# Row sums of 1024 floats on one core: two row blocks of 112 and 16 with a store each, and a last row added by two chained pair instructions on VectorE

## Chip, cores, metric

The kernel runs on one core of a Trainium2 chip. The metric is the time of one execution on the device in microseconds (us), lower is better. The profile shows a span that is about 1.8 us shorter than the time of the same execution, so differences of spans and of times can be compared.

## The reference

```python
def setup_inputs():
    batch, seq, dim = 32, 512, 1024
    return {"x": np.random.randn(batch, seq, dim).astype(np.float32)}

def reference(x):
    return np.sum(x, axis=-1).astype(np.float32)
```

That is 16,384 rows of 4 KB: 67.1 MB to read and 64 KB to write. Every element is added once, so the kernel is a test of how steadily one core can load.

## The kernel before

The rows are cut into four blocks. In a block each of the 128 partitions owns 32 consecutive rows, so the rows of neighbouring partitions lie 32 x 4 KB = 128 KB apart in memory. A load brings 16 rows a partition (64 KB in one piece from each partition's rows, 8 MB in all) into one of three buffers. VectorE sums 16 rows in one instruction. After each of the first three blocks, ScalarE's queue issues a store of 32 sums a partition (128 bytes).

```python
BLOCKS = (32, 32, 32, 32)
G = 16
ACT_ROWS = 6
CUT = 640
# ... pools: three buffers of 16 rows for x; one buffer for each result
    for b, n in enumerate(BLOCKS):
        x_b, out_b, res = block(done * P, n)
        final = b == len(BLOCKS) - 1
        whole = n - G if final else n
        c = 0
        while c < whole:
            m = min(G, whole - c)
            xt = xpool.tile([P, G * D], F32, tag="xt", name="xt")
            nc.sync.dma_start(out=xt[:, 0 : m * D], in_=x_b[:, c * D : (c + m) * D])
            a = ACT_ROWS if done + c + m == full else 0
            rows_dve(xt, res, 0, m - a, c)
            rows_act(xt, res, m - a, a, c + m - a)
            c += m
        if not final:
            nc.scalar.dma_start(out=out_b, in_=res)
        done += n
```

The last 16 rows come in pieces of 8, 4, 2 and 1 rows and the last row in pieces of 640 and 384 elements, so that little work is left when the last byte lands. VectorE and ScalarE share the rows of each piece. The end of the last row:

```python
    nc.vector.tensor_reduce(
        out=tail[:, D : D + 1], in_=tail[:, 0 : CUT // 2], axis=X, op=ADD
    )
    sum_act(tail[:, CUT // 2 : CUT], tail[:, D + 1 : D + 2])
    nc.vector.tensor_reduce(
        out=res[:, n - 1 : n], in_=tail[:, CUT : D + 2], axis=X, op=ADD
    )
    nc.sync.dma_start(out=out_b, in_=res)
```

`pairs_dve` (already used for the row before the last) is one VectorE instruction that adds the first half of a piece to the second half, sums the results and adds a start value: it covers n elements in n/2 steps (for the row of 1024 elements before the last the trace shows 692 ns).

Of the kernel before, what the change touches and what calls it, by code (L numbers as in the profile page):

```python
# [1 line left out]

# [4 lines left out]

F32 = mybir.dt.float32
ADD = mybir.AluOpType.add
COPY = mybir.ActivationFunctionType.Copy  # L10
X = mybir.AxisListType.X

BLOCKS = (32, 32, 32, 32)
G = 16
ACT_ROWS = 6
CUT = 640


@with_exitstack
def row_sums(  # L20
    ctx: ExitStack,
    tc: tile.TileContext,
    x: bass.AP,
    out: bass.AP,
):
    nc = tc.nc
    P = nc.NUM_PARTITIONS

    x_flat = x.flatten_outer_dims()
    R, D = x_flat.shape  # L30
    C = R // P
    assert R % P == 0 and sum(BLOCKS) == C
    out_flat = out.rearrange("a (b c) -> (a b c)", c=1)

    xpool = ctx.enter_context(tc.tile_pool(name="x", bufs=3))
    rpool = ctx.enter_context(tc.tile_pool(name="res", bufs=1))
    tail = rpool.tile([P, D + 2], F32, name="tail")

    def rows_dve(xt, res, j, n, c):
        nc.vector.tensor_reduce(  # L40
            out=res[:, c : c + n],
            in_=xt[:, j * D : (j + n) * D].rearrange("p (j d) -> p j d", d=D),
            axis=X,
            op=ADD,
        )

    def sum_act(v, acc):
        nc.scalar.activation(out=v, in_=v, func=COPY, accum_out=acc)  # L48

    def rows_act(xt, res, j, n, c):  # L50
        for i in range(n):
            sum_act(xt[:, (j + i) * D : (j + i + 1) * D], res[:, c + i : c + i + 1])

    def pairs_dve(xt, a, b, first, acc):
        h = (a + b) // 2
        nc.vector.tensor_tensor_reduce(  # L56
            out=xt[:, a:h], in0=xt[:, a:h], in1=xt[:, h:b], scale=1.0, scalar=first,
            op0=ADD, op1=ADD, accum_out=acc,
        )

    def block(r0, n):
        x_b = x_flat[r0 : r0 + P * n].rearrange("(p c) d -> p (c d)", p=P)
        out_b = out_flat[r0 : r0 + P * n].rearrange("(p c) -> p c", p=P)
        return x_b, out_b, rpool.tile([P, n], F32, name=f"res{r0}")

    full = C - G
    done = 0
# [18 lines that stand above are left out]
    cuts = [0, 8, 12, 14, 15]  # L86
    for i, k in zip(cuts, cuts[1:]):
        nc.sync.dma_start(out=xt[:, i * D : k * D], in_=x_b[:, (c + i) * D : (c + k) * D])
    last = (n - 1) * D
    nc.sync.dma_start(out=tail[:, 0:CUT], in_=x_b[:, last : last + CUT])  # L90
    nc.sync.dma_start(out=tail[:, CUT:D], in_=x_b[:, last + CUT : last + D])

    for i, k in zip(cuts[:2], cuts[1:3]):
        h = (k - i + 1) // 2
        rows_dve(xt, res, i, h, c + i)
        rows_act(xt, res, i + h, k - i - h, c + i + h)
    i = cuts[2]
    rows_dve(xt, res, i, 1, c + i)
    rows_act(xt, res, i + 1, 1, c + i + 1)
    i += 2  # L100
    pairs_dve(xt, i * D, (i + 1) * D, 0.0, res[:, c + i : c + i + 1])
    nc.vector.tensor_reduce(  # L102
        out=tail[:, D : D + 1], in_=tail[:, 0 : CUT // 2], axis=X, op=ADD
    )
    sum_act(tail[:, CUT // 2 : CUT], tail[:, D + 1 : D + 2])
    nc.vector.tensor_reduce(  # L106
        out=res[:, n - 1 : n], in_=tail[:, CUT : D + 2], axis=X, op=ADD
    )
    nc.sync.dma_start(out=out_b, in_=res)


def kernel(tc: tile.TileContext, x: bass.AP, out: bass.AP):
    row_sums(tc, x, out)
    tc.close()
    tc.compile()  # L115



    sp = mybir.EngineType.SP
    entry, body = None, None  # L120
    for blk in tc.nc.m.functions[0].blocks:
        ops = [i for i in blk.instructions if i.engine == sp]
        if entry is None:
            entry = blk
        elif any(i.opcode == "DMACopy" for i in ops):
            body = blk
            break
    code = list(body.instructions)
    load = next(i for i in code if i.engine == sp)
    assert load.opcode == "DMACopy" and not load.sync_info.on_wait  # L130
    code.remove(load)
    body.instructions = code
    code = list(entry.instructions)
    at = next(k for k, i in enumerate(code) if i.engine == sp and i.opcode == "Drain")
    code.insert(at, load)
    entry.instructions = code


# [1 line left out]
_INS = ['x']  # L140
_OUTS = [((32, 512), 'float32')]


# [23 lines left out]
```

## Time and profile before

| | before |
|---|---|
| time, median of 3 runs | 162.77 us (162.54 to 163.09) |
| span of the profiled execution | 161.35 us (its time: 163.13) |
| bytes loaded over the span | 416 GB/s |
| VectorE / ScalarE busy | 77% / 10% |
| load queue, share of the 16 DMA engines' span | 97.2% |

The page of the kernel before: its head, its busy engines and its DMA queues. q1 is the queue of the loads and the last store, q10 the queue on which ScalarE issues; the columns of a queue are packets, MB, and the time its packets took as a share of 16 engines' span.

```profile
span 161.3 us, 116 instructions
...
DVE 123.5 (77%) x14; ACT 15.8 (10%) x29; POOL 0.2 (0%) x4
...
q1 hardware_dynamic: 2016, 67.13, 97.2%
q10 hardware_dynamic: 432, 0.05, 0.2%
```

The loads leave the DMA engines idle for under 3% of the span, and VectorE is idle for a quarter of it. So the loads bound the kernel, and a change can only win what lies between the packets, before the first, or after the last.

VectorE's timeline of the kernel before, from the fourth load on (start, duration, engine, line, operation, tiles and shapes, and in brackets the idle time before it and what ended it):

```profile
80.01 17.22 DVE L40 TENSOR_REDUCE res<-xt 128x16 f32<-128x16384 f32 x1 [2.15 <-DMA xt<-in_x_dram]
99.57 17.22 DVE L40 TENSOR_REDUCE res<-xt 128x16 f32<-128x16384 f32 x1 [2.34 <-DMA xt<-in_x_dram]
119.30 17.22 DVE L40 TENSOR_REDUCE res<-xt 128x16 f32<-128x16384 f32 x1 [2.51 <-DMA xt<-in_x_dram]
138.73 18.46 DVE L40 TENSOR_REDUCE res<-xt 128x10 f32<-128x10240 f32 x4 [2.21 <-DMA xt<-in_x_dram]
```

Each of these starts when a load lands, so the differences of the starts are the times between landings: 19.56, 19.73 and 19.43 us here, and 19.34 to 19.37 for the loads before.

The end of the timeline of the kernel before:

```profile
157.95 0.47 ACT L48 ACTIVATE tail<-tail 128x320 f32<-128x320 f32 x1 [0.97 <-DMA tail<-in_x_dram]
157.95 0.49 DVE L102 TENSOR_REDUCE tail<-tail 128x1 f32<-128x320 f32 x1
158.33 0.19 ACT L48 ACTIVATION_READ_ACCUMULATOR tail<-tail 128x1 f32 x1
158.55 0.55 DVE L106 TENSOR_REDUCE res<-tail 128x1 f32<-128x386 f32 x1
159.13 0.35 SPq L109 DMA_DIRECT2D out_dram<-res  x1
```

and of its chain of waits, the work that ended last, in order of time (start, duration, what):

```profile
119.46 38.47 DMA tail<-in_x_dram
157.93 0.02 issue
157.95 0.47 ACT tail L48
158.42 0.10 ACTq L115
158.52 0.02 issue
158.55 0.55 DVE res L106
```

### The profile page before, as it was taken

The page shows a single profiled execution, that of the slowest core. Times are in us where ns is not written, and L with a number is a line of the kernel's source. Part 1 is how long each engine was busy: PE and PEld are TensorE (multiplying, and loading weights), DVE is VectorE, ACT ScalarE, POOL GpSimd, SP SyncE. Part 2 cuts the span into 40 slices and gives each one's busy share as a digit, 9 for nine tenths or more (in the row PEclk, how much of TensorE's full clock was granted, in tenths as well). Part 3 has the DMA queues.
Part 4 walks back from the last instruction along what each step waited for, and adds up shares of the span by engine and source line. Part 5 has one row for each costly group of instructions (what it writes and reads, how often), then busy time and mean ns, then how long its engine had stood idle before and what let it go on. Part 6 is the DMA issues. An engine that isn't in the chain of part 4 may idle for free.

```text
span 161.3 us, 116 instructions
## 1 busy us (share of the span) xinstructions
DVE 123.5 (77%) x14; ACT 15.8 (10%) x29; POOL 0.2 (0%) x4
## 2 busy tenths in 40 slices
DVE  0000059997799959999499994999949998699994
ACT  0000000000000000000000000000000000891881
POOL 0000000000000000000000000000000000000000
DMA  7995995996995995996996996997979969999991
GB/s 260 520 520 260 520 520 260 520 520 260 520 520 260 520 520 260 521 521 260 521 520 260 520 520 260 521 456 326 521 309 471 520 260 520 390 391 449 406 407 44
DMA packets 2448, 67.18 MB, mean 416 GB/s; under 512 B 784, under 2 KB 912, under 8 KB 1168
## 3 DMA queue, kind: packets, MB, share of 16 engines
q1 hardware_dynamic: 2016, 67.13, 97.2%
q10 hardware_dynamic: 432, 0.05, 0.2%
HBM read 67.11 MB, written 0.07 MB: 416 GB/s over the span
## 4 chain that ended last, share of the span: by engine, by line
DMA 76%; DVE 22%; ACT 0%; issue 0%; ACTq 0%
DMA xt<-in_x_dram 39%; DMA tail<-in_x_dram 24%; DVE res L40 21%; DMA out_dram<-res 14%; DVE res L106 0%; ACT tail L48 0%; ACTq L115 0%
## 5 line engine op out<-in xcount | busy, mean ns | idle before, releaser
L40 DVE TENSOR_REDUCE res<-xt 128x16 f32<-128x16384 f32 (+4 forms) x10 | 121.8, 12203 | 35.4 <-DMA xt<-in_x_dram 35.4
L48 ACT ACT_TABLE_LOAD x1 | 1.3, 1283 | 137.0 <-DVE res L40 137.0
L48 ACT ACTIVATE xt<-xt 128x1024 f32<-128x1024 f32 x13 | 13.6, 1045 | 4.8 <-DMA xt<-in_x_dram 4.8
L48 ACT ACTIVATION_READ_ACCUMULATOR xt<-xt 128x1 f32 x13 | 2.4, 186 | 0.0
L56 DVE CUSTOM_DVE_ANT_0 xt<-xt 128x512 f32<-128x512 f32 x1 | 0.7, 692 | 0.0
L106 DVE TENSOR_REDUCE res<-tail 128x1 f32<-128x386 f32 x1 | 0.6, 554 | 0.1
L48 ACT ACTIVATE tail<-tail 128x320 f32<-128x320 f32 x1 | 0.5, 470 | 1.0 <-DMA tail<-in_x_dram 1.0
L102 DVE TENSOR_REDUCE tail<-tail 128x1 f32<-128x320 f32 x1 | 0.5, 486 | 0.0
L48 ACT ACTIVATION_READ_ACCUMULATOR tail<-tail 128x1 f32 x1 | 0.2, 187 | 0.0
L151 POOL MEMSET const-uint8-127<- 128x1 uint8 x1 | 0.1, 103 | 0.0
L151 POOL MEMSET const-bfloat16-1.0<- 128x1 bf16 x1 | 0.1, 102 | 0.0
L151 POOL MEMSET const-float32-0.0<- 128x1 f32 x1 | 0.1, 99 | 0.2 <-issue 0.2
L151 POOL MEMSET const-float32-1.0<- 128x1 f32 x1 | 0.1, 99 | 0.0
L56 DVE DVE_READ_ACCUMULATOR2_ANT res<- 128x1 f32 x1 | 0.1, 84 | 0.0
## 6 DMA issues: line engine op xcount, KB each, us to landing
xt<-in_x_dram SPq DMA_DIRECT2D x1, 4096.0 KB, 31.6
xt<-in_x_dram SPq DMA_DIRECT2D x1, 2048.0 KB, 36.1
xt<-in_x_dram SPq DMA_DIRECT2D x1, 1024.0 KB, 38.1
xt<-in_x_dram SPq DMA_DIRECT2D x1, 512.0 KB, 38.9
tail<-in_x_dram SPq DMA_DIRECT2D x1, 320.0 KB, 38.5
tail<-in_x_dram SPq DMA_DIRECT2D x1, 192.0 KB, 38.6
xt<-in_x_dram SPq DMA_DIRECT2D x7, 41.0
out_dram<-res ACTq DMA_DIRECT2D x3, 16.0 KB, 22.2
```

The source lines that it names most:

```text
L40: nc.vector.tensor_reduce(out=res[:, c : c + n], in_=xt[:, j * D : (j + n) * D].rearrange("p (j d) -> p j d", d=D), axis=X, op=ADD,)
L48: nc.scalar.activation(out=v, in_=v, func=COPY, accum_out=acc)
L56: nc.vector.tensor_tensor_reduce(out=xt[:, a:h], in0=xt[:, a:h], in1=xt[:, h:b], scale=1.0, scalar=first, op0=ADD, op1=ADD, accum_out=acc,)
L102: nc.vector.tensor_reduce(out=tail[:, D : D + 1], in_=tail[:, 0 : CUT // 2], axis=X, op=ADD)
L106: nc.vector.tensor_reduce(out=res[:, n - 1 : n], in_=tail[:, CUT : D + 2], axis=X, op=ADD)
L151: nc = _bacc.Bacc("TRN2", target_bir_lowering=False, num_devices=1)
```

## The change

The intent: fewer and larger stores (112 sums a partition, 448 bytes, in place of three times 128 bytes), and a last row that only VectorE works on, with the first pair instruction between the two landings and the second after the last one. The row before the last goes to ScalarE.

```diff
-BLOCKS = (32, 32, 32, 32)
+BLOCKS = (112, 16)
 G = 16
 ACT_ROWS = 6
-CUT = 640
+CUT = 576
+EARLY = 1
...
-    tail = rpool.tile([P, D + 2], F32, name="tail")
+    part = rpool.tile([P, 1], F32, name="part")
...
-    last = (n - 1) * D
-    nc.sync.dma_start(out=tail[:, 0:CUT], in_=x_b[:, last : last + CUT])
-    nc.sync.dma_start(out=tail[:, CUT:D], in_=x_b[:, last + CUT : last + D])
+    last = 15 * D
+    for i, k in ((0, CUT), (CUT, D)):
+        nc.sync.dma_start(
+            out=xt[:, last + i : last + k],
+            in_=x_b[:, c * D + last + i : c * D + last + k],
+        )
 
-    for i, k in zip(cuts[:2], cuts[1:3]):
-        h = (k - i + 1) // 2
+    for i, k in zip(cuts[:3], cuts[1:4]):
+        h = (k - i) // 2
         rows_dve(xt, res, i, h, c + i)
-        rows_act(xt, res, i + h, k - i - h, c + i + h)
-    ...  (rows 12 to 15: ScalarE's and VectorE's halves, as shown above)
+        rows_act(xt, res, i + h, h, c + i + h)
+    rows_act(xt, res, 14, 1, c + 14)
+    pairs_dve(xt, last, last + CUT, 0.0, part)
+    pairs_dve(xt, last + CUT, last + D, part, res[:, c + 15 : c + 16])
     nc.sync.dma_start(out=out_b, in_=res)
```

The rest of the diff lets EARLY loads be issued ahead of the start barrier; with EARLY = 1 that is what the kernel did before. With 112 rows a partition, neighbouring partitions' rows now lie 448 KB apart instead of 128 KB. (The last 16 rows of a partition are a block of their own, so in the pieces at the end they lie 64 KB apart.)

More of the change, by code (lines that the diff above doesn't have):

```diff
@@ L88, in row_sums @@
         nc.sync.dma_start(out=xt[:, i * D : k * D], in_=x_b[:, (c + i) * D : (c + k) * D])
-    last = (n - 1) * D
-    nc.sync.dma_start(out=tail[:, 0:CUT], in_=x_b[:, last : last + CUT])
-    nc.sync.dma_start(out=tail[:, CUT:D], in_=x_b[:, last + CUT : last + D])
-    for i, k in zip(cuts[:2], cuts[1:3]):
-        h = (k - i + 1) // 2
-        rows_dve(xt, res, i, h, c + i)
-        rows_act(xt, res, i + h, k - i - h, c + i + h)
-    i = cuts[2]
-    rows_dve(xt, res, i, 1, c + i)
-    rows_act(xt, res, i + 1, 1, c + i + 1)
-    i += 2
-    pairs_dve(xt, i * D, (i + 1) * D, 0.0, res[:, c + i : c + i + 1])
-    nc.vector.tensor_reduce(
-        out=tail[:, D : D + 1], in_=tail[:, 0 : CUT // 2], axis=X, op=ADD
-    )
-    sum_act(tail[:, CUT // 2 : CUT], tail[:, D + 1 : D + 2])
-    nc.vector.tensor_reduce(
-        out=res[:, n - 1 : n], in_=tail[:, CUT : D + 2], axis=X, op=ADD
-    )
+    last = 15 * D
[6 more added lines that the diff above has]
+        h = (k - i) // 2
+        rows_dve(xt, res, i, h, c + i)
+        rows_act(xt, res, i + h, h, c + i + h)
+    rows_act(xt, res, 14, 1, c + 14)
+    pairs_dve(xt, last, last + CUT, 0.0, part)
+    pairs_dve(xt, last + CUT, last + D, part, res[:, c + 15 : c + 16])
     nc.sync.dma_start(out=out_b, in_=res)
@@ L128 @@
     code = list(body.instructions)
-    load = next(i for i in code if i.engine == sp)
-    assert load.opcode == "DMACopy" and not load.sync_info.on_wait
-    code.remove(load)
+    loads = [i for i in code if i.engine == sp][:EARLY]
+    for load in loads:
+        assert load.opcode == "DMACopy" and not load.sync_info.on_wait
+        code.remove(load)
     body.instructions = code
@@ L134 @@
     at = next(k for k, i in enumerate(code) if i.engine == sp and i.opcode == "Drain")
-    code.insert(at, load)
+    code[at:at] = loads
     entry.instructions = code
```

## The prediction

> **What bounds it now.** The 16 DMA engines. The page's queue part gives the load queue 97.2% of 16 engines' span; VectorE is busy 77%, ScalarE 10%. The packet records of the trace show 64 KB load packets of 2418 ns at the least, back to back: 4.19 MB an engine at that rate is 154.8 us of the 161.3 us span (estimate from those records). The rest: [...]0.8 us of longer first packets, 1.2 us of longer packets and gaps, and the end after the last landing (about 158.45): in the timeline the last reduce runs 158.55 to 159.10, its store is issued at 159.13, the span ends at 161.3. VectorE's 17.22 us for each 16-row load fits in the 19.4 us between landings. The bytes loaded don't change, so nothing large can be won.
>
> **What the change does.**
> 1. Three stores of 128-byte packets during the loads become one of 448-byte packets. The Trainium skill ("DMA: Bandwidth & Descriptors", Issuing engines are not separate DMA queues) says that DMAs issued from ScalarE interleave with others on the same 16 engines; the packet records agree: store packets of 13 ns between load packets, 8 an engine for each store[...]. That is 0.3 us an engine for three stores; one of larger packets should cost 0.1 to 0.15. Gain 0.15 to 0.2 us, on the critical path.
> 2. The end. Before, the last piece lands at about 158.45 and VectorE starts at 158.55, held by ScalarE's half of the 640 piece (157.95 to 158.52), and takes 0.55 us. After: the pairs on 288 elements, about 0.46 us (estimate: 692 ns for 512, so 1.04 ns an element and 160 fixed), fit between the two landings; the pairs on 224 need 0.40. The result is ready 0.15 to 0.2 us earlier.
> 3. The trap: the 112-row store stands in ScalarE's order behind its six rows and waits for VectorE's 10-row reduce (10.82 us, ends near 149.5). ScalarE's rows of the last 16, begun at 148.47 before, begin near 149.9. It has eight rows at 1.05 us, the last landing near 157.1, and ends near 158.4, half a microsecond before VectorE: off the critical path, with little slack.
> 4. Rows of neighbouring partitions lie 448 KB apart instead of 128 KB; the contiguous run stays 64 KB. The fifth and sixth loads now show packets of 2450 to 2456 ns against 2418 to 2426, which I can't explain; if it is the addresses, this may move half a microsecond either way.
> 5. ScalarE's table load leaves the end of the kernel: it was not on the chain.
>
> **Sum.** 162.77 - 0.17 - 0.18, about 162.4 us; range 161.7 to 163.0 (the three runs of before spread 162.54 to 163.09). Faster by over 2%: 0.01; within 2%: 0.98; slower: 0.01.
>
> **What would show it.** Load queue still about 97% busy; last landing 0.1 to 0.5 us earlier; landings 19.35 to 19.7 us apart; from the last landing to the last store's issue 0.45 us in place of 0.65; the big store landing within about 8 us of an issue near 149.9, before the last loads end; ScalarE's last read ending before VectorE's last pairs.
>
> **What would make it wrong.** The new row stride slows or speeds the packets of all loads (each 1% is 1.5 us); ScalarE, started late, ends last; the big store lands after the last loads and holds the end of the program; the second pairs wait for the first's sum longer than the two landings are apart.

The first packets start 0.99 to 1.51 us after the start of the span, and the three stores landed 23.9, 22.2 and 12.5 us after their issue.

## More of the kernel before

The chain does not run through the last piece of 384 elements (landed at 158.40) but through the piece before it, of 640: landed at 157.93, ScalarE's half of it, then the last reduce. From that landing to the issue of the last store are 1.20 us; from the landing of the last piece they are 0.73.

## The result

| | before | after |
|---|---|---|
| time, median of 4 runs | 162.66 us (162.46 to 163.09) | 162.46 us (162.34 to 162.61) |
| span of the profiled execution | 161.35 us | 160.83 us |
| load queue's share | 97.2% | 97.2% |
| rate over the span | 416 GB/s | 418 GB/s |

The ratio is 0.9985 with a 95% interval of 0.9962 to 1.0008. A ratio is the mean time of one kernel's fast runs over the mean of the other's fast runs of the same rounds, so it is not quite the ratio of the medians. The changed kernel run once more later, over five rounds on another chip, gave 0.9979 (0.9964 to 0.9994), so the gain is real: 0.2 to 0.35 us of 162.7.

The page after, the same parts:

```profile
span 160.8 us, 116 instructions
...
DVE 122.7 (76%) x14; ACT 16.1 (10%) x29; POOL 0.2 (0%) x4
...
q1 hardware_dynamic: 2016, 67.12, 97.2%
q10 hardware_dynamic: 144, 0.06, 0.1%
```

VectorE's timeline after, from the fourth load on:

```profile
80.06 17.22 DVE L41 TENSOR_REDUCE res<-xt 128x16 f32<-128x16384 f32 x1 [2.14 <-DMA xt<-in_x_dram]
99.42 17.22 DVE L41 TENSOR_REDUCE res<-xt 128x16 f32<-128x16384 f32 x1 [2.14 <-DMA xt<-in_x_dram]
118.76 17.22 DVE L41 TENSOR_REDUCE res<-xt 128x16 f32<-128x16384 f32 x1 [2.12 <-DMA xt<-in_x_dram]
138.11 18.46 DVE L41 TENSOR_REDUCE res<-xt 128x10 f32<-128x10240 f32 x4 [2.13 <-DMA xt<-in_x_dram]
```

The landings are now 19.36, 19.34 and 19.35 us apart. At 138.11 the changed kernel is 0.62 us ahead of the kernel before (138.73), and at the end of the span it is 0.52 us ahead. So in this pair of profiles the whole gain was made in the loads five to seven, before the new end began.

The timeline after: the big store on ScalarE's queue and what follows it, and the end.

```profile
149.02 0.37 ACTq L83 DMA_DIRECT2D out_dram<-res  x1
149.51 1.06 ACT L49 ACTIVATE xt<-xt 128x1024 f32<-128x1024 f32 x1 [3.69 <-DVE res L41]
...
157.50 0.46 DVE L57 CUSTOM_DVE_ANT_0 xt<-xt 128x288 f32<-128x288 f32 x1 [0.92 <-DMA xt<-in_x_dram]
157.75 0.19 ACT L49 ACTIVATION_READ_ACCUMULATOR xt<-xt 128x1 f32 x1
157.88 0.08 DVE L57 DVE_READ_ACCUMULATOR2_ANT part<- 128x1 f32 x1
158.01 0.45 DVE L57 CUSTOM_DVE_ANT_0 xt<-xt,part 128x224 f32<-128x224 f32 x1
158.39 0.08 DVE L57 DVE_READ_ACCUMULATOR2_ANT res<- 128x1 f32 x1
158.53 0.35 SPq L104 DMA_DIRECT2D out_dram<-res  x1
```

The chain of waits after, its end:

```profile
118.49 38.86 DMA xt<-in_x_dram
157.35 0.03 issue
157.38 0.02 DVEq L57
157.40 0.10 issue
157.50 0.46 DVE xt L57
157.95 0.02 DVE part L57
157.97 0.04 issue
158.01 0.45 DVE xt L57
```

Again the chain starts at the landing of the last row's first piece (157.35), and from there to the issue of the last store are 1.18 us. Before it was 1.20. The new end is not a shorter chain. It gains only because the first piece is smaller and so lands sooner: its packets took 93 to 94 ns against 102, eight of them on each engine, which is 0.07 us. Counted from the landing of the last piece, the store was issued after 0.66 us in place of 0.73. But even this was lost again after the last store: from the landing of the last piece to the end of the span both profiles have 2.95 us. Why is told under no_stores.

ScalarE did what was feared and no more: its store waited for VectorE until 149.02, its next row began at 149.51, and its last read ended at 157.94, half a microsecond before VectorE's last read. The big store landed 6.6 us after its issue.

### The profile page after: what moved, and what is told of

Same layout as the page of the kernel before. It is cut to its first block, busy times and chain, and to the rows that moved or that the text cites. A ratio compares the mean times of both kernels' runs of the same rounds, so it can differ in the third digit from the quotient of the medians.

```text
span 160.8 us, 116 instructions
## 1 busy us (share of the span) xinstructions
DVE 122.7 (76%) x14; ACT 16.1 (10%) x29; POOL 0.2 (0%) x4
## 3 DMA queue, kind: packets, MB, share of 16 engines
q1 hardware_dynamic: 2016, 67.12, 97.2%
## 4 chain that ended last, share of the span: by engine, by line
DMA 75%; DVE 22%; SPq 1%; issue 0%; DVEq 0%
DMA xt<-in_x_dram 75%; DVE res L41 21%; SPq L89 1%; DVE xt L57 1%; DVEq L57 0%; DVE part L57 0%; DVEq L110 0%
## 5 line engine op out<-in xcount | busy, mean ns | idle before, releaser
L49 ACT ACTIVATE xt<-xt 128x1024 f32<-128x1024 f32 x14 | 14.6, 1043 | 3.7 <-DVE res L41 3.7
L57 DVE CUSTOM_DVE_ANT_0 xt<-xt 128x288 f32<-128x288 f32 x1 | 0.5, 458 | 0.9 <-DMA xt<-in_x_dram 0.9
L57 DVE CUSTOM_DVE_ANT_0 xt<-xt,part 128x224 f32<-128x224 f32 x1 | 0.5, 451 | 0.0
```

The source lines that it names most:

```text
L49: nc.scalar.activation(out=v, in_=v, func=COPY, accum_out=acc)
L57: nc.vector.tensor_tensor_reduce(out=xt[:, a:h], in0=xt[:, a:h], in1=xt[:, h:b], scale=1.0, scalar=first, op0=ADD, op1=ADD, accum_out=acc,)
```

## How the packets were read

The trace keeps a record of every DMA packet: start, duration, size, queue. I sorted the load packets by start and took them 16 at a time: one packet of each engine, a "round". The mean start of a round to the mean start of the next tells the pace of the engines whatever their order. Undisturbed rounds of 64 KB packets took 2414 to 2415 ns, which is 65536 / 2414.5 = 27.1 GB/s an engine and 434 GB/s for 16. The Trainium skill ("DMA: Bandwidth & Descriptors", Specifications) gives 435 GB/s as the ceiling of the path into the on-chip memory, and the trace agrees with it to 0.2%. So the packets themselves run at the ceiling, and the time is decided by what makes some of them longer.

The mean duration in ns of the 128 packets of each of the loads two to seven (the first load is longer in all of them, about 2500 ns):

| run | distance of partitions' rows | loads 2, 3, 4, 5, 6, 7 |
|---|---|---|
| before | 128 KB | 2422, 2426, 2421, **2456, 2450, 2435** |
| again_before | 128 KB | 2420, 2423, 2418, 2418, 2425, 2429 |
| end_only | 128 KB | 2419, 2421, 2423, **2457, 2439**, 2429 |
| no_stores | 128 KB | 2419, 2420, 2421, 2419, 2421, 2425 |
| after | 448 KB | 2419, 2420, 2419, 2419, 2420, 2423 |
| after_again | 448 KB | 2419, 2419, 2419, 2419, 2421, 2423 |
| blocks_only | 448 KB | 2419, 2420, 2420, 2419, 2423, 2431 |
| three_stores | 448 KB | 2419, 2421, 2418, 2418, 2418, 2419 |
| stride512 | 512 KB | **2442, 2445**, 2421, **2440**, 2422, 2424 |
| one_block | 512 KB | 2420, 2420, 2430, 2419, 2420, 2424 |

A load is eight rounds, so 30 ns more a packet is 0.24 us more a load. Added over its loads, the packets of before are 0.57 us an engine longer than those of after, which is the 0.55 us by which the last load ended earlier after.

## The experiments

Theory 1, the prediction's: what is won is the packet time of the stores and a shorter end. Theory 2 (A in the expectations): the distance between the partitions' rows lengthens the load packets, and the change won by leaving 128 KB. Theory 3 (B in the expectations): the long packets are chance, in any kernel. The runs of each group were made on one chip together. "Before" in a ratio is the kernel before in the same rounds.

### First group: repeat and take apart

**again_before**: the kernel before, unchanged.

> The kernel before, run as if it were a change. In the profile of before the packets of loads five to seven were longer (means 2456, 2450, 2435 ns) than in the profile after (2419 to 2423), which is all of the 0.55 us by which the last load ended earlier there. Theory A (row stride): they are longer in every run of the row layout of before, so here again about 2450. Theory B (chance of one execution): here they are back near 2420, or other loads show it, and the last load ends about 156.4 us after the first packet. Time: ratio 1.000, and its interval tells what this method can resolve.

Measured: 162.73 us (162.41 to 163.05), ratio 1.0001 (0.9985 to 1.0017). The long packets were not there. So they don't come with the old layout in every execution: theory 2 in its strict form falls. The interval also shows that a group of this kind resolves some 0.25 us and not the 0.1 us of a single term.

**blocks_only**: the kernel before with only the blocks changed.

```diff
-BLOCKS = (32, 32, 32, 32)
+BLOCKS = (112, 16)
```

> The blocks of 112 and 16 with the old end of 640 and 384 elements shared with ScalarE. If my sum is right (stores 0.17 us, end 0.1 us by the profile after), this is 0.1 to 0.2 us faster than before, ratio 0.999. If the row stride is what counts (theory A), the load packets are at 2420 ns throughout and it is 0.4 to 0.6 us faster, ratio 0.997. ScalarE's late start (near 149.5) should not show at the end: its seven rows end near 157.

Measured: 162.58 us (162.38 to 162.77), ratio 0.9993 (0.9979 to 1.0006). Between the two expectations, and not told apart by time. The chain of waits of this run, with the old end in it:

```profile
118.35 38.89 DMA tail<-in_x_dram
157.24 0.02 issue
157.26 0.47 ACT tail L48
```

Its last store was issued at 158.44, again 1.20 us after the landing of the piece of 640.

**end_only**: the changed kernel with the old blocks.

```diff
-BLOCKS = (112, 16)
+BLOCKS = (32, 32, 32, 32)
```

> The old four blocks of 32 with the new end. If the end is worth what the profile after shows, the stretch from the last landing to the issue of the last store is 0.58 us against 0.67, and the time is 0.1 us less, ratio 0.9995. Theory A wants long packets in loads five to seven here, theory B does not.

Measured: 162.58 us (162.46 to 162.97), ratio 0.9994 (0.9978 to 1.0011). A gain of the end alone is not resolved. In this profile the long packets are back (2457 and 2439 ns), in a kernel with the old row distance and the new end. Its chain has the first piece's landing at 157.69 and the store's issue at 158.89: 1.20 us.

**three_stores**: the changed kernel with three early stores of 32, 32 and 48 columns in place of one of 112.

```diff
-        if not final:
-            nc.scalar.dma_start(out=out_b, in_=res)
+            if not final and c in STORES:            # STORES = (32, 64, 112)
+                p = STORES[STORES.index(c) - 1] if STORES.index(c) else 0
+                nc.scalar.dma_start(out=out_b[:, p:c], in_=res[:, p:c])
```

> The changed kernel with its one store of 112 columns cut into three of 32, 32 and 48 columns at the places of before, same row stride. Theory 'fewer stores pay': about 0.1 us slower than the changed kernel (packets of 13, 13 and about 15 ns, 8 of each an engine: 0.33 us against 0.20), so 0.15 us faster than before, ratio 0.999. Theory A: the stride stays, so load packets stay near 2420 ns and the time stays at that of the changed kernel, ratio 0.9985 or less.

Measured: 162.58 us (162.41 to 162.70), ratio 0.9991 (0.9978 to 1.0004). Three stores with the new row distance are as quick as one (blocks_only has one and gave the same median), and the load packets stayed at 2418 to 2421 ns. So the number of stores is not what makes the packets of before long. The rounds give the cost of the stores themselves: 64 KB rounds with a 128-byte store packet in them took 2423 to 2424 ns against 2414 to 2415, so 9 to 10 ns each, eight times a store: 0.08 us a store, 0.23 us for three. In the changed kernel the 8 KB rounds with a 448-byte store packet took 326 to 327 ns against 306 to 307: 20 ns each, eight times, 0.16 us. One large store for three small ones saves 0.07 us.

### Second group: amplify and take away

**no_stores**: the kernel before without its three early stores. Its output is wrong, which doesn't matter for the time.

```diff
-        if not final:
-            nc.scalar.dma_start(out=out_b, in_=res)
```

> The kernel before without its three early stores: wrong on purpose, three quarters of the output are never written. It gives the most that dropping stores can win. By the profiles taken so far a 64 KB packet with a 128-byte store packet beside it takes 2424 ns from start to start against 2414 to 2415 alone, so a store costs its eight packets an engine some 10 ns each, 0.08 us, and three cost 0.24 us. Theory 'stores are paid in packet time': ratio 0.9985. Rival 'stores hide between the load packets': ratio 1.000. Old row stride: theory A (stride makes long load packets) expects some rounds over 2430 ns in loads five to seven, theory B (chance) as often as not none.

Measured: 162.68 us (162.48 to 162.94), ratio 1.0010 (0.9998 to 1.0022): no gain at all. The last load did end earlier, 156.24 us after its first packet against 156.51 in again_before. But it was lost at the end: from the end of the first piece's packets to the issue of the last store took 1.78 us against 1.70, and from there to the end of the span 2.38 against 2.22. The first difference lies before the landing: from the first piece's landing to the issue are 1.20 us in both. The second lies after the last store's landing, which came 1.44 and 1.43 us after its issue. From then on the span went on for 0.94 us against 0.79.

The trace's records of SyncE's instructions, which the views leave out, show why. At the end of the program SyncE steps through its waits for the DMA semaphores in a fixed order, about 0.06 us each. In before and again_before the last store's semaphore stands in the last of these waits, and 0.79 us follow its landing. In after, after_again, stride512 and blocks_only one more wait comes behind it (0.88 us), in no_stores two more (0.94), in many_stores three (0.98). So a kernel with fewer DMAs can lose here what it wins elsewhere, when its last store uses a semaphore that stands earlier in this order: the changed kernel lost 0.08 us in this way, about as much as its new end had won, and no_stores lost 0.15 us. The packet time of the stores was won in the trace, but the timed runs show no gain from it on this chip, where the kernel before was also at its best (162.36 to 162.81).

**many_stores**: the changed kernel with 13 early stores.

```diff
-        if not final:
-            nc.scalar.dma_start(out=out_b, in_=res)
+            if not final:
+                w = 8 if c < n else m
+                for p in range(c - m, c, w):
+                    nc.scalar.dma_start(out=out_b[:, p : p + w], in_=res[:, p : p + w])
```

> The changed kernel with two stores of 8 columns (32 bytes a partition) after each of the first six loads and one of 16 columns after the seventh, 13 early stores in place of one. If every store packet costs its engine about 10 ns whatever it carries: 13 x 8 x 10 ns = 1.04 us against 0.16 to 0.20 us for the one of 448 bytes, so 0.85 us slower than the changed kernel, 0.6 to 0.7 slower than before, ratio 1.004. If stores hide: ratio 0.999. If a store below some size costs much more, several us.

Measured: 165.51 us (165.34 to 165.65), ratio 1.0184. A miss, and for a reason that I had not allowed for. The rounds with a 32-byte store packet took 2420 ns, only 5 to 6 ns more than without. The 3 us came from a wait, as the DMA queue's own waits show (who waited on what: us in total, times, longest):

```profile
SPq L77 <- DMA out_dram<-res: 59.6, 2, 36.2
```

and VectorE's timeline shows the hole it left:

```profile
99.39 17.22 DVE L41 TENSOR_REDUCE res<-xt 128x16 f32<-128x16384 f32 x1 [2.15 <-DMA xt<-in_x_dram]
121.43 17.22 DVE L41 TENSOR_REDUCE res<-xt 128x16 f32<-128x16384 f32 x1 [4.82 <-DMA xt<-in_x_dram]
```

The kernel has eight semaphores for its DMAs and takes them in turn; with so many stores a load's semaphore was last used by a store that had not landed, and the queue held the load back until it had. The Trainium skill ("DMA: Bandwidth & Descriptors", Anatomy of one DMA, which is about DMAs issued from GpSimd but says this of the DMA engines as such) says that a wait happens on the issuing sequencer before dispatch and not in the DMA engines. This trace agrees for loads issued from SyncE: the sixth load was issued near 99.6, all engines together ran dry for 1.5 us (2.0 us on the mean of them), and the first packets after the hole took 3.1 us in place of 2.4. The kernel before has such a wait too: the first piece of its last row was issued at 119.46, when the second store had landed at 119.44. There some 38 us of loads were still queued ahead, so the engines did not run dry. As a measure of store cost by time the run is void; the rounds stand.

**act4**: the changed kernel with four rows of the seventh load on ScalarE in place of six.

```diff
-ACT_ROWS = 6
+ACT_ROWS = 4
```

> The changed kernel with ScalarE taking 4 rows of the seventh load in place of 6, so that VectorE's reduce of that load has 12 rows and ends 2.1 us later, near 151.1, and with it the big store's issue. In the profile after, ScalarE's last read ended at 157.94, 0.5 us before VectorE's last read. If ScalarE's queue behind the store is the trap that the prediction described, its eight rows now begin near 151.6 and end near 160.1, which is 1.6 us after VectorE's end of the changed kernel: 164.1 us, ratio 1.009. Rival: VectorE's own late rows carry the end (they end near 158.7, then two pair instructions): 0.9 to 1.2 us later. If the late start does not matter: ratio 0.999.

Measured: 163.59 us (163.52 to 163.65), ratio 1.0066 (1.0053 to 1.0079), so 1.1 us slower than the changed kernel's 162.46. The rival was right:

```profile
151.03 0.37 ACTq L83 DMA_DIRECT2D out_dram<-res  x1
151.45 1.06 ACT L49 ACTIVATE xt<-xt 128x1024 f32<-128x1024 f32 x1 [2.51 <-DVE res L41]
...
158.51 0.45 DVE L57 CUSTOM_DVE_ANT_0 xt<-xt 128x288 f32<-128x288 f32 x1
158.65 0.19 ACT L49 ACTIVATION_READ_ACCUMULATOR xt<-xt 128x1 f32 x1
```

VectorE reaches its first pair instruction at 158.51 with no idle time before it, while ScalarE is done at 158.84, before VectorE's second pair instruction ends at 159.45. The build had put one of ScalarE's last rows ahead of the store, so its queue was shorter than I had counted, and this run does not show a case in which the late ScalarE ends last. It shows that the two engines are balanced to half a microsecond.

**one_block**: the changed kernel with one block of 128 rows and a single store at the end.

```diff
-BLOCKS = (112, 16)
+BLOCKS = (128,)
```

> The changed kernel with a single block of 128 rows a partition: no early store at all, one last store of 512 bytes a partition. Saves the 0.16 to 0.20 us of the 448-byte store packets in the stream, ScalarE starts its last rows at the landing (near 148) instead of 149.5, and the last store's packets grow from 10 to some 22 to 28 ns, eight an engine, so 0.1 to 0.15 us more at the end: net 0 to 0.1 us faster than the changed kernel, ratio to before 0.998 to 0.9985. The candidate to beat both, by an amount at the edge of what can be resolved. Row stride is 512 KB here: theory A expects the load packets to differ again, theory B does not.

Measured: 163.22 us (162.96 to 163.62), ratio 1.0044 (1.0032 to 1.0056): 0.7 us slower than before, where I expected the best version. Two things differ from the changed kernel besides the absent store: the row distance is 512 KB, and the last store carries 512 bytes a partition (its packets took 27 ns against 10, and from its issue to the end of the span were 2.49 us against 2.30). In its profile the load packets are near 2420 ns but for the fourth load (2430). The last load ended 156.67 us after the first packet, and the last engine 0.5 us behind the mean of the 16. The third group takes the row distance alone.

### Third group: the row distance alone

**after_again**: the changed kernel, unchanged.

> The changed kernel once more, five rounds, for a tighter ratio. By the profiles so far the change is worth: stores 0.24 us before against 0.16 to 0.20 after, so 0.05; the end nothing in the chain (from the last packet of the last row's first piece to the issue of the last store 2.65 to 2.69 us in both ends) and 0.08 from a first piece of 576 in place of 640 elements; chance long packets the rest. Sum 0.13 us: ratio 0.9992. The prediction on record wanted 0.35 us: ratio 0.998.

Measured: 162.45 us (162.36 to 162.66), ratio 0.9979 (0.9964 to 0.9994); the kernel before took 162.78 us (162.46 to 163.19) in these rounds. The 2.65 to 2.69 us in this expectation are a slip of mine: packet times from the first packet were set against times from the start of the span, and the right figures are 1.66 and 1.68. That the two ends are alike stays true. My sum of 0.13 us was too small for this chip, where the kernel before was slower and more scattered than on the others. The load packets are at 2419 to 2423 ns again.

**after_no_store**: the changed kernel without its early store. Its output is wrong, which doesn't matter for the time.

```diff
-        if not final:
-            nc.scalar.dma_start(out=out_b, in_=res)
```

> The changed kernel without its early store: wrong on purpose. In the kernel before, leaving out three stores took 0.27 us off the end of the last load in the profile but came out 0.16 us slower than before in time; the last store then took 0.16 us longer from issue to the end of the span. Theory C: a core that has not stored yet pays more for its first store, so here too the gain is lost: issue to end 2.38 us or more, ratio to before 0.9995 to 1.001. Theory D (chance in that profile): the 0.16 us of store packets are gained, ratio 0.998 to 0.9985.

Measured: 162.35 us (162.31 to 162.56), ratio 0.9974 (0.9959 to 0.9989), 0.1 us below after_again in the same rounds, which the intervals do not separate. From the last store's issue to the end of the span took 2.37 us against 2.29, so half of the store's 0.16 us came back as a loss, as in no_stores. Theory C (a core's first store costs more) is wrong: the last store landed 1.43 us after its issue, against 1.42 in after_again, and many_stores, with 13 early stores, also took 2.39 us to the end. The rest is SyncE's waits after that landing: 0.94 us against 0.88.

**stride512**: the changed kernel with 512 KB in place of 448 KB between the partitions' rows, and the same stores of 112 and 16 columns.

```diff
-BLOCKS = (112, 16)
+BLOCKS = (128,)
...
-        if not final:
-            nc.scalar.dma_start(out=out_b, in_=res)
+        head = n - G if final else n
+        nc.scalar.dma_start(out=out_b[:, 0:head], in_=res[:, 0:head])
...
-    nc.sync.dma_start(out=out_b, in_=res)
+    nc.sync.dma_start(out=out_b[:, c:n], in_=res[:, c:n])
```

> The changed kernel with neighbouring partitions' rows 512 KB apart in place of 448 KB and all else alike: same instructions in the same order, an early store of 448 bytes a partition from ScalarE, a last one of 64. The kernel with one block was 0.72 us slower than before: if its row stride did that, this one is as slow: ratio 1.003 or more, and the spread of the engines' ends again near 0.6 us between the mean and the last. If its single store of 512 bytes at the end did it (0.14 us more packet time, 0.2 us more from issue to end), this one is at the changed kernel's time: ratio 0.999.

Measured: 163.08 us (163.03 to 163.22), ratio 1.0016 (1.0000 to 1.0032). All six runs lie above all six of after_again (162.36 to 162.66) on the same chip, and every engine has the same instructions in the same order. VectorE's timeline for its second to fourth loads:

```profile
41.59 17.22 DVE L41 TENSOR_REDUCE res<-xt 128x16 f32<-128x16384 f32 x1 [2.27 <-DMA xt<-in_x_dram]
61.13 17.22 DVE L41 TENSOR_REDUCE res<-xt 128x16 f32<-128x16384 f32 x1 [2.32 <-DMA xt<-in_x_dram]
80.51 17.22 DVE L41 TENSOR_REDUCE res<-xt 128x16 f32<-128x16384 f32 x1 [2.16 <-DMA xt<-in_x_dram]
```

The second and third in after_again:

```profile
41.20 17.22 DVE L41 TENSOR_REDUCE res<-xt 128x16 f32<-128x16384 f32 x1 [2.12 <-DMA xt<-in_x_dram]
60.55 17.22 DVE L41 TENSOR_REDUCE res<-xt 128x16 f32<-128x16384 f32 x1 [2.13 <-DMA xt<-in_x_dram]
```

In stride512 there are 19.50 us before the first of its lines and 19.54 to the next, then 19.38, where after_again has 19.34 and 19.35 for the first two: the same kind of long loads as in the kernel before. The last load ended 157.06 us after the first packet against 156.30 in after_again. Of this 0.76 us, 0.65 is in the mean of the 16 engines' ends, and 0.11 is that the last engine was 0.40 us behind the mean in place of 0.29; a load has landed only when its slowest engine is done. So the row distance changes the time: theory 2 holds for 512 KB. Two things go with it that this run does not separate: the rows of the output lie 512 bytes apart too, and the last 16 rows lie 512 KB apart and not 64. Neither can explain the long loads two, three and five, which ended before any store was issued and before the last rows. One_block has the same distance and was as slow in time, but its profile shows only one slightly longer load. Against after_again it lost 0.37 us by the end of the last load, 0.2 of them because its last engine was further behind the mean, and 0.20 us from the issue of its larger last store to the end. So how 512 KB costs time also differs from execution to execution.

**early3**: three loads issued ahead of the start barrier.

```diff
-EARLY = 1
+EARLY = 3
```

> The changed kernel with its new setting EARLY at 3: the first three loads are issued ahead of the start barrier, in place of one. The second load's packets follow the first's without a gap already (rounds of 2415 ns right after the first load), so nothing should come of it: ratio as the changed kernel's, 0.999. If the first load's long packets (3.1 us in place of 2.4) are due to late descriptors of the others: up to 0.7 us faster.

Measured: 162.44 us (162.31 to 162.62), ratio 0.9977 (0.9962 to 0.9992): the changed kernel's time. Nothing to win there, as expected. No correct version was found that beats the changed kernel.

### All runs together, by row distance

Profiles are single executions. The timed runs are more:

| distance | kernels | timed runs | range, us | above 162.77 us |
|---|---|---|---|---|
| 128 KB | before (37), again_before, end_only, no_stores | 54 | 162.36 to 163.19 | 16 |
| 448 KB | after, after_again, blocks_only, three_stores, after_no_store, early3 | 34 | 162.31 to 162.77 | 0 |
| 512 KB | stride512 (one_block has another end) | 6 | 163.03 to 163.22 | 6 |

162.77 is the highest run of the middle line. Act4 and many_stores are left out because they have other ends or waits. The groups differ in their early stores (none, one or three) and in their ends (old and new), and neither sorts the runs: with the old distance the high runs occur with the old end, with the new end (162.96, 162.97) and without early stores (162.94); with the new distance they occur with no kernel. The lowest runs of the old and the new distance in the same rounds differ by 0 to 0.15 us. Chip by chip the sign is the same: in the rounds of the first group 7 of 23 runs at the old distance lie above 162.77 and none of 12 at the new; in those of the third group 6 of 11 and none of 18. The change did little to the best case and took away the slower executions. That the old distance makes long packets likely and not certain is the reading that fits; it rests on the timed runs and on two profiles of four with long packets against none among those of the new distance (the highest mean there is 2431, in blocks_only). It is not shown as strictly as the pair at 448 and 512 KB: the closest pair for it, end_only and three_stores, which differ in the row distance and hardly in anything else, had the same median of 162.58 us and differ only in end_only's two slow runs of six. No run keeps the changed kernel and sets its distance to 128 KB with one store. Theory 3, chance that no layout changes, does not fit either.

## Why the prediction was right, and where its reasons were not

The number held: 162.4 us predicted, 162.46 measured, in the range of 161.7 to 163.0, and 0.35 us of gain predicted against 0.20 in the medians of the first comparison and 0.33 in those of the second. The bound was read correctly: the loads' queue stayed at 97.2%, and nothing large was to be won.

1. **The stores (0.15 to 0.2 us predicted): mis-sized.** That a store packet stands between load packets on the same engine was right, as the skill's section cited there says. The prediction took each packet's recorded 13 ns as its cost, and guessed 0.1 to 0.15 us for the large store. The rounds show 9 to 10 ns for 128 bytes and 20 for 448: 0.23 us against 0.16, so 0.07 us. This is read from the packets; no timed run resolves it.
2. **The end (0.15 to 0.2 us predicted): the step that failed.** The prediction assumed that the first pair instruction fits between the two landings, and that the last landing starts the second. In the trace the first starts 0.15 us after its landing and ends at 157.96, about when the last piece has landed (near 157.9), and the second then takes 0.45 us in place of 0.40. From the first piece's landing to the last store's issue are 1.18 us, against 1.20 before. The old chain had ScalarE's half in the same place. From the last landing to the issue, where the prediction wanted 0.45 us in place of 0.65, they are 0.66 in place of 0.73. What is left is the smaller first piece, 0.07 us, and SyncE's additional wait after the last store takes it back: from the last landing to the end of the span are 2.95 us before and after.
3. **ScalarE's trap: right, in size too.** Start at 149.5 (149.9 predicted), end half a microsecond before VectorE. act4 showed VectorE and not ScalarE to end last when the balance is moved, so the trap itself was not sprung.
4. **The row distance: named, and left without a size.** "This may move half a microsecond either way" was the term that mattered most. 512 KB in place of 448 costs 0.6 us; 128 KB lets executions up to half a microsecond slower appear, which 448 KB does not show. With 0.07 us from item 1 and nothing from item 2, this is what must fill the gap to the measured gain; for 128 KB that is argued from the runs together and not shown by a single pair, and how much it gives depends on the chip and the execution.
5. **ScalarE's table load: harmless, but not as described.** It did not stand at the end of the kernel before, where it began at 136.97, ahead of ScalarE's first row. After, it begins at 138.18, and ScalarE's first row 0.75 us later than before (139.47 and 138.72). ScalarE then waits for its store until 149.02 anyway, so nothing on the chain is delayed.

So the sum was right partly by luck: a term without a size made up for one that was sized about twice too large and one that came to nothing. The Trainium skill has a row on this very thing ("DMA: Bandwidth & Descriptors", Latency and other measured facts): copies between tensors in HBM (the chip's main memory) with a row pitch of 512 KiB ran at 207 GB/s and one of 4 MiB at 103, against 214 at full rate, with aliasing of memory channels as an unverified inference. I had not looked it up when I predicted. Stride512 took 0.4% longer than after_again (163.08 to 162.45), where the page has 3%.

## What to carry to other kernels

When loads already run at the ceiling, a change of blocking is also a change of the distance between concurrent streams in memory: check it separately, with a kernel whose instructions are identical, before crediting stores or instructions with a gain. At an end with two landings, count the chain from the first landing as well as from the last: shortening the work after the last piece wins nothing when the piece before it starts the longer chain, and look at what the program still does after its last store has landed. A difference of a few tenths of a microsecond between two profiles can be one slow execution; look at whether the slow packets come back in a repeat.

## What the Trainium skill lacked or had wrong

- "DMA: Bandwidth & Descriptors", Latency and other measured facts, gives the loss by row pitch for copies between tensors in HBM at 512 KiB and more. It lacks loads into on-chip memory with long contiguous runs (64 KB here): 512 KB cost 0.6 us of 162.5 against 448 KB, and at 128 KB 16 of 54 executions were above the slowest of 34 at 448 KB. That the loss can come and go from one execution to the next is on no page.
- The same page, Specifications, sets 512 bytes as the least transfer for line rate. It has no cost of a small store packet between large loads: 5 to 6 ns an engine for 32 bytes, 9 to 10 for 128, 20 for 448. These runs show no step at 512: packets of 448 bytes took 25 ns in the records and packets of 512 took 27, though the first stood among loads and the second after them.
- No page says how far the engines of one load lie apart and whether this lag is kept from load to load. In after_again the last engine reported 0.28 us behind the mean in the first load and 0.26 in the last, in stride512 0.39 and 0.39, and in three_stores, at 448 KB, 0.50 and 0.47; in one_block it grew from 0.36 to 0.52 us at the fourth load.
- No page gives what SyncE's waits at the end of a kernel cost once the last store has landed: 0.79 us to the end of the span with that store's semaphore in the last of the waits, and about 0.06 us more for each wait that stands behind it.
